# Hybrid attention block: tiles of one-pass matmuls moved to one address residue, a second accumulator in the second norm, and ScalarE's order written out at the end

## The chip, the cores and the metric

The kernel runs on one core of one Trainium2 chip. The metric is the device time of one execution in microseconds (us), as the median over several runs.

## The reference

One layer of a streaming encoder on 1024 frames (T) of 1024 features (D), all in float32:

```python
h = rmsnorm(x, norm1_g)
qa, ka, va, qb, kb, vb = split(h @ w_in)             # 8 heads of 64 in each group
ya = chunked_attention(qa, ka, va, rel_bias)          # softmax over a band of 9 chunks of 64 frames
yb = stick_breaking_attention(qb, kb, vb)             # causal, no softmax
x = x + concat(rmsnorm(ya, norm_a_g), rmsnorm(yb, norm_b_g)) @ w_out
u = causal_depthwise_conv3(rmsnorm(x, norm2_g) @ w_ffn_in, conv_w) + conv_b   # 2 x 2816 columns
gate, val = split(u)
x = x + (silu(gate) * val) @ w_ffn_out
return rmsnorm(x, final_g)
```

`rmsnorm(x, g)` is x / sqrt(mean of x² over the features + 1e-6) × g.

## The kernel before

**Layout and products.** Activations lie transposed, features on the 128 partitions and frames along the free axis: a [1024, 1024] array is 8 tiles of [128, 1024]. Nearly every matrix product is made in three matmuls of the one-pass type fp32r: each operand is split into a rounded high part (copied by ScalarE) and a low part (the rest, subtracted by VectorE or GpSimd, `sub`, L132), and high×high, high×low and low×high are added up in PSUM. The weight piece is the stationary operand (128 columns of it), the activations are the moving one (512 columns). One tile's "product" in the stages below is 4 input tiles × 3 = 12 matmuls into one bank of [128, 512].

**Stages.** 
- *start*: the first norm and the value projection (`all_v`, L506) in seven products p = 1, 2, 5, 6, 7, 3, 4 of a Strassen-like scheme with 48 matmuls each, then the queries and keys of group B in four rounds (`early`, L1255): each round seven products of 12 matmuls.
- *b* and *a*: the two attention groups, with projections in between as filler.
- Output projection (`out_part`, L154) with residual, second norm, and the first up projection.
- *ffn*: the up projection in pairs of column tiles. `up_pair` (L1875) makes, for f = 3 to 21, the seven products a11, s1, s2, a12, s3, s4, a22 of 12 matmuls, while VectorE and ScalarE finish the previous pair (conv taps at L1899, bias and last tap at L1893) and make the pieces of the next one. The down projection follows (L2386, 70 entries of 12 matmuls), and `last_down` (L2249 ff.) does the last two of 22 feature tiles, the residual and the final norm in three parts of 3, 3 and 2 blocks of 128 frames (`LAST`).

**Where tiles lie.** Tiles come from pools, one after another in each partition's bytes. The long-lived pools `cp`, `wp` and `kp` hold most operands; each stage has a pool of its own behind them. The first tile of all, `cst`, holds 40 columns of constants (160 bytes); the stage pool of *ffn* begins with `conv`, 176 columns (704 bytes: three conv taps, the bias and some columns of zeros); that of *start* begins with the tiles `r0` to `r3`, `l0`, `l1`, then `ms` (64 bytes) and `c`. By these sizes, tiles of `cp`, `wp` and `kp` begin at 192 modulo 256 bytes; in *start* `r0` to `l1` begin at 64 and `c` at 128; in *ffn* everything behind `conv` begins at 128.

**The second norm.** For each half g of the frames and each feature tile d, `out_part` makes the projection, the residual is added, and `norm_part` / `x2_part` squares the tile on ScalarE (L1681, L1686) and adds the squares up: the first goes directly into an accumulator, the others into a temporary that GpSimd adds (L1687). `own = KT - len(accs)` is the last d that goes through GpSimd; with one accumulator in the half that is d = 7. `totals` (L171) sums over the partitions with small matmuls against ones, one group for each accumulator; `root` (L163) takes the square root on ScalarE and the reciprocal on VectorE; `across` (L184) spreads it over the partitions by transposes. Then for each tile VectorE multiplies (L1706), ScalarE copies the high part (L1709) and VectorE subtracts. `second_norm` is a generator: the first `next` does `rstd`, the second the transposes and the first tile, and each further one a tile. The first half is stepped by the loop over d of the second half, with 0, 1, 1, 1, 1, 1, 2, 2 steps; the second half's `rstd` is written at n = 6 in `up_first`'s loop over (ct, k) (L1928), its further steps from n = 10 on.

**Order.** TensorE's order is the one written in the code throughout, as are those of VectorE, ScalarE and GpSimd and of the loads, until `last_down`. There, VectorE and GpSimd still follow the code, and ScalarE's order is left to the scheduler. In `last_down` each part does for d = 0 to 7 the products, an add on VectorE (L2313), the square into one of 1, 2 or 4 accumulators, and for some d a multiplication by the final gain on ScalarE (L2293 in the third part, L2320 in the others). `final` of a part is a generator that runs inside the next part: at d = 2 `rstd` (its root needs an ACT_TABLE_LOAD in the first part), then the transposes, ScalarE's copy of their result (L2270) and VectorE's multiplies (L2284) one by one with an output DMA each. For the third part, VectorE and GpSimd multiply pairs of tiles (L2275).

Of the kernel before, what the change touches and what calls it, by code (L numbers as in the profile page):

```python
# [9 lines left out]
F32 = mybir.dt.float32  # L10
# [6 lines left out]
P = 128  # L17
T = 1024
D = 1024
KT = 8  # L20
G = 2
GW = 512
FF = 2816
NF = FF // P
# [31 lines left out]
LATE_W = ("wo6", "wo7")  # L56
H2_TAGS = {0: ("x6", "x7"), 1: ("x0", "x1"), 2: ("x2", "x3")}

C_G1, C_G2, C_GY, C_GF, C_TB, C_W0, C_W1, C_W2, C_CB = 0, 8, 16, 24, 32, 40, 84, 128, 172
C_N = 216  # L60


def r32(ap):
# [4 lines left out]
def tile_hybrid_block(  # L68
# [13 lines left out]
    nc = tc.nc  # L82
    V, S, PE, GP = nc.vector, nc.scalar, nc.tensor, nc.gpsimd
# [31 lines left out]

    cst = one("cst", "cst", shape=(P, C_W0))
    nc.scalar.dma_start(cst, consts[:, :C_W0])
    conv = {}

    def c1(off):  # L120
        t, off = (cst, off) if off < C_W0 else (conv["t"], off - C_W0)
        return t[:, off : off + 1]

    ident = one("ident", "ident", shape=(P, P))
# [23 lines left out]
    def rows(g):  # L148
        return slice(g * GW, (g + 1) * GW)
# [27 lines left out]
    def rstd(sums, c0, c1, width, rn, name):  # L177

        root(rn[:, c0:c1], totals(sums, c1 - c0, name), width)
# [19 lines left out]
    with tc.tile_pool(name="kp", bufs=2) as kp:  # L199
# [43 lines left out]
        for k in range(KT):  # L243
            a, b = hpair(k, "hT")
# [3 lines left out]
        def all_v():  # L248
# [11 lines left out]

            def own(tag, dt=F32R, shape=(P, T)):
                return pools["sbuf"].tile(list(shape), dt, tag=tag, name=f"v_{tag}", bufs=1)

            w_areas = (
                (area(own("r0"), own("r1")), area(own("r2"), own("r3"))),
# [39 lines left out]
            bring_row(1)  # L305
            nc.sync.dma_start(v_d[0][P:, 4 * T - GW :], consts[:1, C_N:])

# [1166 lines left out]
        with stage("b"):  # L1474
# [11 lines left out]
            for b in range(len(items) + 3):  # L1486
                cur, h = items[b] if b < len(items) else (None, 0)
                step = (RATE_B / 16 if cur else DRAIN) / (1.5 if b < 2 else 3)
                if cur:
                    n = cur.n  # L1490
# [11 lines left out]
                if ending:  # L1502
                    pair, ending = ending, []
                    n = pair[0].n
# [88 lines left out]
        for b in range(len(blocks) + 2):  # L1593
# [6 lines left out]
            if cur and cur.i == 0:  # L1600
                n, p = cur.n, cur.p
# [6 lines left out]
            if b in (2, 3):  # L1608
                g = b - 2
# [14 lines left out]
            if cur and cur.p == 3 and cur.i in (3, 4):  # L1624
                g = cur.i - 3
# [62 lines left out]

        wa = []
        acc0 = kp.tile([P, 2 * GW], F32, tag="v", name="n2_acc0", bufs=4)  # L1690
        accs = {0: [acc0[:, rows(0)]]}
        hp2 = [None] * KT

        def second_norm(g):
# [32 lines left out]
        for g in range(G):  # L1727
            if g == 1:
                at1 = wp.tile([P, 2 * GW], F32, tag="wr", name="n2_at1", bufs=1)
                accs[1] = [at1[:, rows(0)]]  # L1730
            for d in range(KT):
                if (g, d) == (0, 5):
                    up_r = {ct: kp.tile([P, D], F32, tag="v", name=f"up{ct}_r", bufs=4) for ct in (0, NF)}
                    for ct in (0, NF):
                        nc.sync.dma_start(up_r[ct], w_up[ct])
                if g == 0 and d % 2 == 0:
                    wa.append(take(w_late if d > 3 else w_ready))
                for _ in out_part(*wa[d // 2], 0, d, g, "pa"):
                    pass
                flow.emit(x2_chains[d, g])  # L1740
                if (g, d) == (0, 3):
                    fetch(w_late, kp, ("x10", "x11"), 1)
                    flow.drain()
                first = {1: 0, 3: NF}.get(d) if g else None
                if first is not None:
                    first_high(first)
                nc.sync.dma_start(x2_d[d][:, rows(g)], x2[d][:, rows(g)])
                norm_part(d, rows(g), accs[g], kp, f"n2_{g}")
                if first is not None:
                    first_low(first)  # L1750
                for _ in range((0, (0, 1, 1, 1, 1, 1, 2, 2)[d])[g]):
                    next(norms[0])
        a_stage.__exit__(None, None, None)

    with stage("ffn"):
        fp = pools["sbuf"]
        conv["t"] = fp.tile([P, C_N - C_W0], F32, tag="conv", name="conv", bufs=1)

        def at(slot, name, dt=F32):
            pool = wp if slot == "wr" else fp if slot[0] == "s" else cp  # L1760
# [150 lines left out]
        def up_first():  # L1911

            o = {(g, ct): zbank(f"u{ct}_{g}") for g in range(G) for ct in (0, NF)}
            c = {f: (at("s7", f"cg{f}"), at("s8", f"cv{f}")) for f in (0,)}
            raws = [at(t, f"up1_r{i}") for i, t in enumerate(("s9", "s10"))]
            for t, ct in zip(raws, (1, NF + 1)):
                nc.sync.dma_start(t, w_up[ct])
            nc.sync.dma_start(conv["t"], consts[:, C_W0:C_N])
            load_up(2)
            w1 = [[], []]  # L1920

            def weights1(n):
                w1[n] += [piece(raws[n][:, r], f"up1_{n}{i}") for i, r in enumerate(halves)]

            def plain(o, w, k, g, first, last, r=None):
                wh, wl = w
                for i, (a, t) in enumerate(((wh, 0), (wh, 1), (wl, 0))):
                    PE.matmul(  # L1928
                        o, a[:, cols(k if r is None else r)], hp2[k][t][:, rows(g)],
                        start=first and i == 0, stop=last and i == 2,  # L1930
                    )

            n = 0
            for ct in (0, NF):
                for k in range(KT):
                    if n == 6:
                        next(norms[1])
                        weights1(0)
                    if n >= 10:
                        next(norms[1])  # L1940
                    plain(o[0, ct], up_w[ct], k, 0, k == 0, k == KT - 1)
                    n += 1
                S.copy(c[0][ct // NF][:, lo], o[0, ct])
            for _ in norms[1]:
                pass
            weights1(1)
            sums = combine_all("t2")
            for _ in range(3):
                next(sums)
            for i, k in enumerate(K_ORDER[1]):  # L1950
                for ct in (0, NF):
                    plain(o[1, ct], up_w[ct], k, 1, i == 0, i == KT - 1)
            for ct in (0, NF):
                S.copy(c[0][ct // NF][:, hi], o[1, ct])
            done, left = Finish(0, *c[0]), Left(2)
            done.first("g")
            for _ in sums:
                pass
            done.first("v")
            left.whole_high()  # L1960
            done.taps("g")
            left.make("s1")
            left.whole_low()
            done.taps("v")
            done.silu()
            left.make("s2")
            left.make("s4")
            c[1] = (at("s7", "cg1"), at("s8", "cv1"))

            def product_1(n, bank):  # L1970
                os = [bank(f"u1_{n}{g}") for g in range(G)]
                for k in range(KT):
                    for g in range(G):
                        plain(os[g], w1[n][k // 4], k, g, k == 0, k == KT - 1, k % 4)
                return lambda: [S.copy(c[1][n][:, rows(g)], os[g]) for g in range(G)]

            copy = product_1(0, med)
            for _ in combine_all("t3"):
                pass
            done.gate()  # L1980
            left.high("s4")
            left.high("s2")
            copy()
            done = Finish(1, *c[1])
            left.low("s4")
            left.low("s2")
            done.first("g")
            left.make("s3")
            product_1(1, pj)()
            for _ in combine_all("t4"):  # L1990
                pass
            load_up(3)
            done.taps("g")
            for w in ("s3", "s1", "a22"):
                left.high(w)
            for w in ("s3", "s1", "a22"):
                left.low(w)
            load_up(4)
            return done
# [249 lines left out]
        def last_down(chunk, x2):  # L2249
            accs = [  # L2250
                at(where[1 + i // 2, 2 + i % 2], f"n3_acc{i}") for i in range(4)
            ]
# [5 lines left out]
            def final(c0, c_end):  # L2258
                sl = slice(c0 * P, c_end * P)
                last = accs[: {3: 1, 6: 2, 8: 4}[c_end]]  # L2260
                rstd([a[:, sl] for a in last], c0, c_end, D, rn2, f"n3_{c0}")
                if c_end == KT:
                    for d in range(4, KT):
                        gain(d)
                yield
                n = (c_end - c0) * P
                ob = zbank(f"n3_{c0}_rb")[:, :n]
# [23 lines left out]
            def gain(d):  # L2291
                y = res[d // 4][:, d % 4, :]
                S.activation(y, y, AF.Copy, scale=c1(C_GF + d))  # L2293
# [109 lines left out]
            do()  # L2403
        own_order.__exit__(None, None, None)
        loads_order.__exit__(None, None, None)
        with tc.manual_schedule(engines={V.engine, GP.engine}):
            last_down([2 * NP, 2 * NP + 1], x2n)
    pe_order.__exit__(None, None, None)

# [1 line left out]
def _layout(inputs):  # L2411
    import numpy as np

    def a(name):
        return np.asarray(inputs[name])

    def cols(v):
        return v.reshape(-1, P).T

    def tiles(w):  # L2420
# [9 lines left out]
    conv_w = a("conv_w")[0]  # L2430
# [1 line left out]
        [  # L2432
            cols(a("norm1_g")[0]), cols(a("norm2_g")[0]), cols(a("norm_a_g")[0]),
            cols(a("norm_b_g")[0]), cols(a("final_g")), np.broadcast_to(rel[:, -1], (P, 8)),
            cols(conv_w[0]), cols(conv_w[1]), cols(conv_w[2]), cols(a("conv_b")[0]),
            np.zeros((P, GW), np.float32),
        ],
        axis=1,
    )
# [32 lines left out]
```

## Time and profile before

| | us |
|---|---|
| median of 3 runs | 1217.43 |
| lowest, highest | 1216.38, 1219.96 |
| the profiled execution | 1217.9 |
| its span | 1216.2 |

Mean granted TensorE clock in the profiled execution: 0.996 of full speed. In the profile, PE is TensorE's matmuls and PEld its weight loads, DVE VectorE, ACT ScalarE, POOL GpSimd, SP the engine that issues most DMAs; L and a number is a line of the kernel. A row of the chain of work has the start, the time and the instruction group that stood on the path; a row of a timeline has the start, the time, engine, line, operation, output and inputs, and in brackets the idle time ahead of it and who ended that.

### The profile page before, as it was taken

Reading aid. Unit: us, or ns where it says so; the run is one execution under the profiler, and the core shown is the slowest. Engines: PE = TensorE matmul, PEld = TensorE weight load, DVE = VectorE, ACT = ScalarE, POOL = GpSimd, SP = SyncE. Lnnn points to the kernel's source line nnn. Section 1 sums busy time; section 2 is a strip of 40 time slices with the busy share of each in tenths; the row PEclk is TensorE's granted clock in tenths of the full one; section 3 lists DMA queues with packets and bytes.
Section 4 is the critical chain, followed back from the end, with each engine's and each line's share of the span. In section 5 each row is a group of like instructions: output and inputs, shape, how many; then the busy total and the mean of one; then the engine's idle time right before and its main releaser. Section 6 shows DMA issues by size and latency. Waiting matters only on the chain.

```text
span 1216.2 us, 17043 instructions
## 1 busy us (share of the span) xinstructions
PE 1195.9 (98%) x6252; PEld 984.3 (81%) x6252; DVE 927.5 (76%) x1382; ACT 685.3 (56%) x1252; POOL 161.9 (13%) x163
## 2 busy tenths in 40 slices
PE   9999999999999999999999999999999999999997
PEld 6788888888878778787888888888888888888886
DVE  7957649878666767468997777768677779979885
ACT  7865436766667667334665554555555555444425
POOL 0001031102211111342000000000000023132035
PEclk9999999999999999999999999999999999999998
DMA  9467577777478831142132222132221295520003
GB/s 329 136 210 265 177 236 197 217 182 187 144 182 253 227 110 53 38 153 107 39 112 92 87 70 99 58 105 71 85 87 70 85 369 237 190 88 1 1 1 139
DMA packets 73793, 166.91 MB, mean 137 GB/s; under 512 B 7783, under 2 KB 23271, under 8 KB 73710
## 3 DMA queue, kind: packets, MB, share of 16 engines
q1 hardware_dynamic: 73566, 165.81, 43.1%
q8 instruction: 49, 0.80, 0.3%
q14 instruction: 34, 0.28, 0.1%
q10 hardware_dynamic: 144, 0.02, 0.0%
HBM read 118.60 MB, written 47.20 MB: 136 GB/s over the span
## 4 chain that ended last, share of the span: by engine, by line
PE 88%; DVE 6%; ACT 3%; DMA 1%; issue 1%; POOL 0%; SPq 0%; DVEq 0%; ACTq 0%
PE u_c L1875 9%; PE u_a L1875 9%; PE u_e L1875 9%; PE dz L2386 8%; PE u_b L1875 5%; PE dm L2386 4%; PE dj L2386 4%; PE v_x L506 4%; PE pb L154 3%; PE pa L154 3%; PE k_p L154 3%; PE v_y L506 3%; PE yb L1011 3%; PE tpb L997 3%; PE q_p L154 3%; PE yy L1144 2%
## 5 line engine op out<-in xcount | busy, mean ns | idle before, releaser
L970 DVE TENSOR_TENSOR_SCAN acts<-zb,first 128x128 f32<-128x128 f32 (+7 forms) x64 | 86.5, 1351 | 17.6 <-ACT zb L979 17.4
L1899 DVE SCALAR_TENSOR_TENSOR vt<-cv,conv,vt 128x1023 f32<-128x1023 f32 (+1 forms) x44 | 58.3, 1325 | 2.2 <-ACT vt L1893 1.5
L1899 DVE SCALAR_TENSOR_TENSOR gt<-cg,conv,gt 128x1023 f32<-128x1023 f32 (+1 forms) x44 | 57.4, 1305 | 1.5 <-ACT gt L1893 0.7
L132 POOL TENSOR_TENSOR dx_0wl<-dr,dx_0wh 128x512 fp32r<-128x512 f32 x1 | 1.4, 1357 | 414.6 <-ACT dx_0wh L2142 414.6
L979 ACT ACTIVATE zb<-zb 128x128 f32<-128x128 f32 (+7 forms) x64 | 41.0, 640 | 26.1 <-PE zb L962 26.1
L1089 ACT ACTIVATE pa<-sa,sta 128x640 f32<-128x640 f32 (+4 forms) x64 | 42.7, 668 | 18.1 <-DVE sta L1080 14.6
L1893 ACT ACTIVATE gt<-cg,conv 128x1024 f32<-128x1024 f32 x22 | 27.4, 1244 | 39.9 <-DVE cg L1767 39.8
L1001 ACT COPY tb<-tpb 128x128 f32<-128x128 f32 (+3 forms) x96 | 43.0, 484 | 6.2 <-PE tpb L997 5.5
L1125 ACT COPY pta<-tpa 128x512 f32<-128x512 f32 (+3 forms) x80 | 36.9, 483 | 13.3 <-PE tpa L1121 13.1
L997 PE MATMUL tpb<-ident,acts 128*128 128x128 f32 x288 | 43.3, 277 | 0.0
L1080 DVE TENSOR_REDUCE sta<-sa 128x1 f32<-128x640 f32 (+4 forms) x64 | 41.8, 655 | 1.3
L1764 DVE TENSOR_TENSOR up_r<-up_r 128x512 f32<-128x512 f32 x60 | 41.3, 688 | 0.8
L1121 PE MATMUL tpa<-ident,pa 128*128 128x128 f32 x240 | 37.9, 277 | 1.1 <-ACT pta L1125 1.1
L997 PEld LDWEIGHTS tpb<-ident,acts 128*128 128x128 f32 x288 | 33.0, 140 | 6.4 <-issue 2.6
L1077 DVE TENSOR_TENSOR sa<-sa,bias 128x256 f32<-128x256 f32 (+1 forms) x64 | 26.4, 414 | 11.0 <-PE sa L1062 7.8
L1121 PEld LDWEIGHTS tpa<-ident,pa 128*128 128x128 f32 x240 | 27.9, 140 | 7.9 <-issue 2.6
L2063 ACT COPY u_b<-u_a 128x512 f32<-128x512 f32 x19 | 10.8, 571 | 38.6 <-PE u_a L1875 38.6
L1144 PE MATMUL yy<-pta,v 128*64 128x256 f32 (+1 forms) x288 | 29.7, 349 | 0.0
L1687 POOL TENSOR_TENSOR n_acc<-n_acc,n_sq 128x384 f32<-128x384 f32 (+2 forms) x24 | 25.6, 1065 | 28.9 <-ACT n_sq L1686 28.1
L1011 PE MATMUL yb<-tb,dv 128*64 128x128 f32 x448 | 29.2, 273 | 0.0
L1764 DVE TENSOR_TENSOR dr<-dr,dr 128x512 f32<-128x512 f32 x40 | 28.7, 739 | 0.0
L154 PE MATMUL pb<-yh,wo_h 128*128 128x512 f32 x64 | 27.0, 421 | 1.8 <-DVE x L1219 1.8
(1400 smaller groups left out, 4011.0 us busy)
## 6 DMA issues: line engine op xcount, KB each, us to landing
up_r<-in_w_up_dram SPq DMA_DIRECT2D x44, 512.0 KB, 3.5
act<-vt SPq DMA_DIRECT2D x22, 512.0 KB, 2.6
dr<-in_w_dn_dram SPq DMA_DIRECT2D x20, 512.0 KB, 7.0
dr<-act SPq DMA_DIRECT2D x20, 512.0 KB, 7.9
wv<-in_w_v_dram SPq DMA_DIRECT2D x16, 256.0 KB, 5.4
xin<-in_xT_dram SPq DMA_DIRECT2D x16, 256.0 KB, 5.4
row<-in_x_rows_dram SPq DMA_DIRECT2D x16, 256.0 KB, 2.6
raw<-in_w_in_dram SPq DMA_DIRECT2D x8, 512.0 KB, 5.2
```

Source lines behind the costliest of these rows:

```text
L154: PE.matmul(o, w[:, sl], t[:, rows(g)], start=first and i == 0, stop=last and i == 2,)
L506: PE.matmul(bank[j], t[:, cols(j)], w, start=p in (1, 5) and k == 0 and i == 0, stop=k == 3 and i == 2, skip_group_check=True,)
L970: V.tensor_tensor_scan(out=a[:, :w], data0=z, data1=first[:, :w], initial=1.0, op0=ALU.mult, op1=ALU.max,)
L997: PE.transpose(tp[:, cols(b)], self.a[h][:, cols(b0 + b)], ident)
L1001: mine.append(flow.add(on_s(m * P, lambda o=o, tp=tp: S.copy(o, tp))))
L1011: PE.matmul(yy[HS[h], :], (d if j else v)[:, off : off + 64], self.at[h][:, self.c0[h] + j * P : self.c0[h] + (j + 1) * P], start=j == 0, ...
L1121: PE.transpose(tp[:, cols(b)], self.pr[src][:, cols(c)], ident)
L1144: PE.matmul(yy[HS[h], q], v[:, c * P + h * 64 : c * P + (h + 1) * 64], t[:, h], start=j == 0, stop=j == len(parts) - 1, skip_group_check=True,
L1764: eng.tensor_tensor(out=out, in0=a, in1=b, op=ALU.subtract)
L1875: PE.matmul(o, w[:, cols(k)], t, start=start and k == 0 and i == 0, stop=k == 3 and i == 2, skip_group_check=True,)
L1899: V.scalar_tensor_tensor(out=t[:, : T - lag], in0=o[:, lag:], scalar=c1(c + ct), in1=t[:, : T - lag], op0=ALU.mult, op1=ALU.add,)
L2386: PE.matmul(o[m], w[:, cols(m)], t, start=i in (0, 1, 4, 5) and p == ps_[0] and j == 0, stop=p == ps_[-1] and j == 2, skip_group_check=True,)
```

## The change

It does three things.

1. *Placement.* The conv bias moves from the stage's tile to the constants loaded at the start, so `cst` has 88 columns (352 bytes, 192 more) and the stage tile, now `taps`, holds the three taps in a tile of 192 columns (768 bytes), of which 132 are loaded. In *start* a tile `front` of 128 bytes that nothing reads or writes stands ahead of `r0`. By the sizes, tiles of `cp`, `wp` and `kp` then begin at 128 modulo 256; in *start* `r0` to `l1` at 128 and `c` at 192; in *ffn* everything behind `taps` at 128. In the other stages tiles keep their distances.
2. *Second norm.* Each half has two accumulators, so d = 7's square goes directly into the second one, and `totals` does two groups of matmuls. The first half is stepped 1, 1, 1, 1, 1, 1, 1, 2 times over d, and the second half's `rstd` is written at n = 5.
3. *The end.* ScalarE's order in `last_down` is the one written. Gains 4 and 5 of the third part stand ahead of its `rstd`, 6 and 7 behind it (before, all four behind it).

```diff
-C_G1, C_G2, C_GY, C_GF, C_TB, C_W0, C_W1, C_W2, C_CB = 0, 8, 16, 24, 32, 40, 84, 128, 172
-C_N = 216
+C_G1, C_G2, C_GY, C_GF, C_TB, C_CB, C_W0, C_W1, C_W2 = 0, 8, 16, 24, 32, 40, 88, 132, 176
+C_N = 220
...
+            own("front", F32, (P, 32))
...
-        accs = {0: [acc0[:, rows(0)]]}
+        accs = {0: [acc0[:, rows(i)] for i in range(2)]}
...
-                accs[1] = [at1[:, rows(0)]]
+                accs[1] = [at1[:, rows(i)] for i in range(2)]
...
-                for _ in range((0, (0, 1, 1, 1, 1, 1, 2, 2)[d])[g]):
+                for _ in range((0, (1, 1, 1, 1, 1, 1, 1, 2)[d])[g]):
...
-        conv["t"] = fp.tile([P, C_N - C_W0], F32, tag="conv", name="conv", bufs=1)
+        taps["t"] = fp.tile([P, 192], F32, tag="taps", name="taps", bufs=1)
...
-            nc.sync.dma_start(conv["t"], consts[:, C_W0:C_N])
+            nc.sync.dma_start(taps["t"][:, : C_N - C_W0], consts[:, C_W0:C_N])
...
-                    if n == 6:
+                    if n == 5:
                         next(norms[1])
...
+                if c_end == KT:
+                    gain(4)
+                    gain(5)
                 rstd([a[:, sl] for a in last], c0, c_end, D, rn2, f"n3_{c0}")
                 if c_end == KT:
-                    for d in range(4, KT):
-                        gain(d)
+                    gain(6)
+                    gain(7)
...
-        with tc.manual_schedule(engines={V.engine, GP.engine}):
+        with tc.manual_schedule(engines={V.engine, S.engine, GP.engine}):
             last_down([2 * NP, 2 * NP + 1], x2n)
```

The host's layout of the constants follows the new columns.

More of the change, by code (lines that the diff above doesn't have):

```diff
@@ L117, in tile_hybrid_block @@
     nc.scalar.dma_start(cst, consts[:, :C_W0])
-    conv = {}
+    taps = {}
     def c1(off):
-        t, off = (cst, off) if off < C_W0 else (conv["t"], off - C_W0)
+        t, off = (cst, off) if off < C_W0 else (taps["t"], off - C_W0)
         return t[:, off : off + 1]
@@ L2434, in _layout @@
             cols(a("norm_b_g")[0]), cols(a("final_g")), np.broadcast_to(rel[:, -1], (P, 8)),
-            cols(conv_w[0]), cols(conv_w[1]), cols(conv_w[2]), cols(a("conv_b")[0]),
-            np.zeros((P, GW), np.float32),
+            cols(a("conv_b")[0]), np.zeros((P, C_W0 - C_CB - 2 * NF), np.float32),
+            cols(conv_w[0]), cols(conv_w[1]), cols(conv_w[2]), np.zeros((P, GW), np.float32),
         ],
```

## The prediction

> **What bounds the kernel now.** I read the page first, then the chain of work that ended last stage by stage, and the timelines of TensorE, VectorE and ScalarE where the chain leaves TensorE.
>
> ```profile
> span 1216.2 us, 17043 instructions
> ...
> PE 1195.9 (98%) x6252; PEld 984.3 (81%) x6252; DVE 927.5 (76%) x1382; ACT 685.3 (56%) x1252; POOL 161.9 (13%) x163
> ...
> PE 88%; DVE 6%; ACT 3%; DMA 1%; issue 1%; POOL 0%; SPq 0%; DVEq 0%; ACTq 0%
> ```
>
> TensorE is busy 98% of the span and carries 88% of the chain. So two things can shorten the kernel: each matmul takes less time, or one of the few stretches where the chain runs through VectorE and ScalarE (9% together) gets shorter. The change tries the first in four stages and the second in two places. The profiled execution took 1217.9 us (its span and 1.7 around it), 0.5 above the median of 1217.43; I make the sum against 1217.9 and take it from the median at the end.
>
> **Part 1, the placement.** First, one period of the channel mixer on the chain (start, time, output tile; each piece is one product of 12 matmuls):
>
> ```profile
> 627.87 2.73 PE u_b L1875 x12
> 630.60 2.76 PE u_a L1875 x12
> 633.36 2.76 PE u_c L1875 x12
> 636.12 2.75 PE u_e L1875 x12
> 638.87 2.75 PE u_c L1875 x12
> 641.62 2.73 PE u_a L1875 x12
> 644.35 2.75 PE u_e L1875 x12
> 647.10 2.73 PE u_b L1875 x12
> ```
>
> The products follow each other without a gap: 647.10 − 627.87 = 19.23 us for seven. They differ a little, and the difference follows the code: u_a at 641.62 (a11) takes both operands from tiles of the old pools, u_b (s2) both from the stage's own pool; both take 2.73. u_e (s1, s4) and u_c at 638.87 (a22) take one from each: 2.75. From the tile sizes, the stage's tiles lie 64 bytes off the others modulo 256: its pool and the old ones begin at the same residue, its first tile has 704 bytes, and that is 64 short of three times 256. u_a at 630.60 (a12) has both alike and still takes 2.76, but it comes right after a product at another residue; so does u_c at 633.36, whose right operands are mixed. What alike operands cost with no such change before them, the first product of the up projection shows, where all tiles are of the old pools (start, time, operation):
>
> ```profile
> 553.36 0.39 PE L1928 MATMUL u<-h2h,up_wh 128*128 128x512 f32 x1
> ...
> 556.76 0.39 PE L1928 MATMUL u<-h2h,up_wh 128*128 128x512 f32 x1
> ```
>
> From the first to the sixteenth are 15 intervals in 3.40 us: 226.7 ns each, 2.72 a product. The change makes the stage's first tile 768 bytes (a multiple of 256) and puts every tile of the mixer at one residue, so I price the period at 7 × 2.72 = 19.04 instead of 19.23. Pairs f = 3 to 21 are 19 periods: 0.19 × 19 = **−3.6**. The other end: at 2.73, the price of the best products in the period, 0.12 × 19 = −2.3; if a12 keeps its 2.76 for another reason and s3 too, 0.06 × 19 = −1.1. Nothing else must run faster for this: in these rows the chain stays on TensorE, and VectorE, 76% busy over the span, is not on it. For f = 0 to 2, I count nothing, since the stretch up to 608 waits for VectorE (part 2).
>
> The same holds at the start, where own tiles lie 128 apart from the others:
>
> ```profile
> 51.09 11.45 PE v_y L506 x48
> 62.53 10.90 PE v_x L506 x48
> 73.44 11.19 PE v_y L506 x48
> ...
> 96.45 2.73 PE ea L1255 x12
> ...
> 101.97 2.80 PE eb L1255 x12
> 104.76 2.74 PE ea L1255 x12
> ...
> 113.05 2.77 PE ec L1255 x12
> ```
>
> Here the same 48 matmuls take 10.90 when both operands are in the old pools (product 3) and 11.45 and 11.19 when the weights' pieces are in own tiles (7 and 4). The `early` products show 2.74 and 2.80 beside each other, and seven of them 113.05 + 2.77 − 96.45 = 19.37. After the change six take 2.72; the seventh reads its low pieces in `c`, which ends 64 bytes off, so about 2.75 as above: 19.07. Four heads' rounds: 0.30 × 4 = **−1.2**. Of `all_v`, products 7 and 4 give about 0.3 each, **−0.6** (for 7, whose 11.45 holds a wait too, I take no more than for 4). What the products ahead of 51 would give I count at nothing, because VectorE sets the pace there:
>
> ```profile
> 45.00:50.00 5.00, 5.00 (x24) 4.14 (x23) 5.00 (x9) 4.16 (x11) 0.00 (x0) 1.00 0.48 148
> ```
>
> The columns are the stretch, its length, then busy time with counts of TensorE's matmuls, weight loads, VectorE, ScalarE and GpSimd: VectorE is busy all 5.00 us. If this cover were not there, two more products would give 0.6.
>
> The down projection, two pieces of the chain, an early one and the last:
>
> ```profile
> 1028.86 13.76 PE dz L2386 x60
> ...
> 1165.87 13.65 PE dz L2386 x60
> ```
>
> Between their starts lie 600 matmuls (50 entries of 12): 137.01 / 600 = 228.4 ns. At 226.7, 840 of them gain 1.4; where pieces are only just ready some of it is lost, and I take **−1.2**. Other fp32r matmuls keep their places: the attention stages' tiles all move by the same 192 bytes, so nothing there changes, and the larger constant load at the start and the conv taps' load are one DMA each before and after. Sum of part 1: −6.6. Bounds: −2.5 (the mixer at −1.1, the rest by half) to −8.
>
> The Trainium skill ("TensorE: Matmul & The Clock Gate", "Step-by-step: what each phase is for") says that streaming operand and weight load have read ports of their own, and that loading weights takes no read bandwidth from the running matmul. By it where the two lie would not matter and part 1 would be zero. The trace does not bear it out: the same 48 matmuls take 10.90 and 11.19.
>
> **Part 2, the second norm.** With two accumulators, the last square of each half goes from ScalarE straight into the second, and GpSimd's last add goes; the totals take 16 small matmul records instead of 8. What bounds it now, on the chain and in the windows:
>
> ```profile
> 535.20 0.79 PE n_ms L171 x8
> ...
> 557.28 0.64 ACT n_sq L1686
> 557.98 1.61 POOL n_at L1687
> 559.64 1.05 PE n_ms L171 x8
> 560.69 4.45 PE u L1928 x12
> 565.14 0.45 PE n_rb L184 x4
> ...
> 565.62 0.76 DVE x L1706
> ...
> 608.21 3.02 PE u_b L1875 x12
> ```
>
> ```profile
> 562.00:564.00 2.00, 2.00 (x7) 1.52 (x6) 1.29 (x2) 1.29 (x3) 0.00 (x0) 0.50 1.05 405
> ```
>
> TensorE gets to the totals, waits until GpSimd has added (557.98 + 1.61 = 559.59), then does four blocks of three matmuls ahead of the transposes; these 12 take 4.45 instead of 12 × 0.227 = 2.72, because the granted clock is down (the last but two column: 0.50 of full speed). VectorE's multiplies follow at 565.62, and from there to 608.21 the chain is VectorE nearly without a gap, so what is won at 565.14 is won at 608. After: the first half's totals cost 0.79 more, while its first step comes one tile earlier and h2 with it, so the up projection starts about 0.5 later (553.9). Five blocks at 0.68 instead of six stand ahead of the totals: 557.3. The square ends at 557.92; the first eight records run before that, the second eight end 0.8 to 1.0 after it, 558.9. Five blocks then stand ahead of the transposes, 3.4: 562.3, at the latest some 0.4 more by a piece of h2 that isn't ready: 562.7. So **−2.4**. If the clock falls as before, 1.73 of it is lost: −0.7. If nothing waits, 562.0: −3.1. The upper end I don't take, since TensorE's small records at 557 to 559 also leave the array idle; the clock I take as granted, since the wait that came before its fall goes.
>
> **Part 3, ScalarE in program order at the end.** `last_down` leaves ScalarE's order to the scheduler now; after, its instructions stand as written. Rows of the timeline (start, time, engine, line; in brackets the idle time before and its releaser):
>
> ```profile
> 1191.15 1.28 ACT L163 ACT_TABLE_LOAD   x1
> ...
> 1192.61 0.51 ACT L1686 ACTIVATE n_sq<-x2n 128x384 f32<-128x384 f32 x1
> ...
> 1193.55 0.48 ACT L2270 COPY n_rbs<-n_rb 128x384 f32<-128x384 f32 x1 [0.43 <-PE n_rb L184]
> ...
> 1194.06 0.61 DVE L2284 SCALAR_TENSOR_TENSOR x2n<-x2n,cst,n_rb 128x384 f32<-128x384 f32 x1 [0.71 <-ACT n_rbs L2270]
> ...
> 1206.07 0.51 ACT L2293 ACTIVATE res<-res,cst 128x256 f32<-128x256 f32 x1
> ...
> 1207.33 0.40 ACT L1681 ACTIVATE n_acc<-res 128x256 f32<-128x256 f32 x1
> 1208.43 0.26 ACT L163 ACTIVATE rn<-n_ms,eps 128x2 f32<-128x2 f32 x1 [0.16 <-PE n_ms L171]
> ```
>
> The scheduler now puts the first part's root, with its table load, ahead of the second part's square of d = 2 (1192.61). As written the root comes behind that square, which can't start before its add: the table load moves from 1191.15 to about 1192.1, +0.95. The copy (1193.55) comes behind the square of d = 3, +0.4. VectorE's multiply waits for this copy, and from 1194.06 on VectorE goes from multiply to add without idling, so 1.35 carries on. In the third part the second root and its copy come behind the gains of d = 2 and 3: a gain starts 0.42 after its neighbour ((1207.33 − 1206.07) / 3 for a gain, a square, a gain), so +0.45 each, +0.9. Given back: the squares of d = 5 to 7 no longer alternate with gains 4 to 6, so the last square comes two gains sooner, −0.9; but gains 4 and 5 now stand ahead of the last root, of which the totals on TensorE hide half, +0.4, and 6 and 7 ahead of the last copy, +0.2. Sum: 0.95 + 0.4 + 0.9 − 0.9 + 0.6 = **+2.0**. Bounds: −0.5, if the first root's delay is taken up by waits for products in the second part and only the end counts; +5, if the table load and each of the four gains and squares named stand on the path in full (1.28 + 8 × 0.45). I take the value between, by the 1194.06 row, on which VectorE waited for ScalarE.
>
> **Sum.** −6.6 − 2.4 + 2.0 = −7.0: 1210.9 for the profiled execution, **1210.4** for the median. About 0.3%, 3.7 us, is what a measurement of this kernel can tell from no change: faster means under 1213.8, slower over 1221.1.
>
> **Rivals.**
> First: the placement pays nothing; the small differences between products come from their order or from who else reads, and alike tiles take 19.23 a period as before. For it: a12, alike, takes 2.76. Against: 10.90 beside 11.19 for the same work, and 226.7 ns in the alike stretch. Then −2.4 + 2.0 = −0.4: 1217.0, no change. That the change misses its aim by a tile that ends elsewhere would come out the same, in part.
> Second: the order at the end costs nothing, because what VectorE waits for is set by the products and their banks anyway, or because fewer alternations repay it. For it: ScalarE idles 0.43 and 0.16 before two of its rows there, so has room. Against: the idle 0.71 on VectorE is ScalarE's. Then −9.0 to −9.5: 1208.2.
> Third, the other side: program order ties VectorE to ScalarE throughout the end. If at each of the 16 steps of parts two and three the next multiply or add waited for a square (0.51) and a gain (0.51), the end would be 16 × 1.02 = 16 longer: −9.0 + 16 = +7, 1224.4. It decides from 12.7 us on (9.0 + 3.7). Against it: an add needs only its product and bank, and a multiply the copy; neither reads a square or gain of its own part.
>
> **How the numbers follow.** The forecast with its terms in their bounds: 0.70; the first rival 0.12, the second 0.15, the third 0.03. The range leaves out the last and most of the first, about 2 in 10 with what lies beyond the bounds: 1207.2 (both the placement at −7.5 and the norm at −2.7, the end at 0) to 1214.4 (the placement at −4, the norm at −1, the end at +2). Faster: 0.70 less a twentieth for terms at their low ends, and 0.15: 0.82. Same: 0.12 and that rest, 0.15. Slower: 0.03.
>
> **What would show it.** Right: u_a to u_e all at 2.72 and periods of 19.04; `early` rounds of 19.1; 60 products of the down projection in 13.60; n_ms on the chain behind a square, not behind GpSimd, and the VectorE multiply of the second half at about 563; the table load at 1192 when counted from the same start of the end, and the end from the first part's table load to the last output about 2 longer, less the shift. Wrong: periods of 19.1 or more; a granted clock of 0.5 again ahead of the transposes; VectorE's multiply in the end waiting no longer than 0.7.

## The result and the profile after

The changed kernel takes 1211.55 us (median of 4 runs, 1211.29 to 1212.13), the kernel before, run again beside it, 1218.43: 6.9 us less, a ratio of 0.9945 with the 95% interval 0.9928 to 0.9962. The forecast was 1210.4 with a range of 1207.2 to 1214.4. The profiled execution of the changed kernel has a span of 1210.4, 5.8 less than the one of before; it took 1212.13, 0.6 above its median, where the one of before lay 0.5 below the 1218.43.

One period of the channel mixer in the chain of waits of the changed kernel (start, time, output tile, line; L1875 is L1877 now):

```profile
623.43 2.72 PE u_b L1877 x12
626.15 2.72 PE u_a L1877 x12
628.87 2.72 PE u_c L1877 x12
631.59 2.72 PE u_e L1877 x12
634.31 2.72 PE u_c L1877 x12
637.03 2.72 PE u_a L1877 x12
639.75 2.72 PE u_e L1877 x12
642.47 2.72 PE u_b L1877 x12
```

Every product takes 2.72, a12 (u_a at 626.15) and s3 (the u_c behind it) too, which took 2.76 before; a period is 642.47 − 623.43 = 19.04. The start of the kernel and the down projection, from the same view:

```profile
50.78 11.17 PE v_y L508 x48
61.95 10.88 PE v_x L508 x48
...
95.52 2.72 PE ea L1257 x12
...
111.84 2.77 PE ec L1257 x12
114.61 2.73 PE ea L1257 x12
...
1157.39 13.60 PE dz L2391 x60
```

A round of `early` is 114.61 − 95.52 = 19.09 instead of 19.37. Its last product, which reads low pieces in the tile `c`, is the only one above 2.73: `c` still lies 64 bytes off. Sixty matmuls of the down projection take 13.60 instead of 13.65.

The second norm, in the chain, with the same places as before:

```profile
530.24 1.68 PE n_ms L171 x16
...
552.21 3.40 PE u L1930 x15
555.61 1.68 PE n_ms L171 x16
557.29 3.57 PE u L1930 x15
...
561.33 0.76 DVE x L1708
...
603.91 3.01 PE u_b L1877 x12
```

GpSimd is gone from the chain: the totals follow fifteen matmuls at once, and the fifteen behind them take 3.57, at a granted clock of 1.00 (twelve took 4.45 before). VectorE's first multiply of the second half comes at 561.33 instead of 565.62.

And the end (timeline of ScalarE, then of TensorE):

```profile
1183.62 1.28 ACT L163 ACT_TABLE_LOAD   x1
...
1186.36 0.46 ACT L2275 COPY n_rbs<-n_rb 128x384 f32<-128x384 f32 x1
...
1201.31 0.42 ACT L1683 ACTIVATE n_acc<-res 128x256 f32<-128x256 f32 x1 [0.30 <-DVE res L2318]
1201.63 0.89 ACT L2298 ACTIVATE res<-res,cst 128x256 f32<-128x256 f32 x2
1202.54 0.26 ACT L163 ACTIVATE rn<-n_ms,eps 128x2 f32<-128x2 f32 x1
```

```profile
1195.90 0.54 PE L184 MATMUL n_rb<-ident,rn 128*128 128x128 f32 x3 [1.52 <-DVE rn L164]
1196.20 4.62 PE L2313 MATMUL dnl<-lx,lw 128*128 128x256 f32 x24
```

These need a common zero: the last 60 matmuls of the down projection begin at 1165.87 before and at 1157.39 after. Counted from there the table load moved from 25.28 to 26.23, +0.95, and the copy from 27.68 to 28.97, +1.3, both as priced. But TensorE now waits 1.52 ahead of the second part's transposes, and the 24 matmuls behind them, which belong to the third part's products, take 4.62. The kernel before had:

```profile
1202.57 0.54 PE L184 MATMUL n_rb<-ident,rn 128*128 128x128 f32 x3 [0.44 <-DVE rn L164]
1202.86 3.11 PE L2308 MATMUL dnl<-lx,lw 128*128 128x256 f32 x24
```

The windows of the changed kernel say why the 24 take longer (stretch, length, busy time of PE, PEld, DVE, ACT and POOL, granted clock, then the DMA engines' share and GB/s):

```profile
1193.50:1195.50 2.00, 0.88 (x7) 0.67 (x6) 0.00 (x0) 1.94 (x6) 1.13 (x2) 1.00 0.22 78
...
1197.50:1199.50 2.00, 2.00 (x11) 2.00 (x11) 1.84 (x4) 0.51 (x3) 0.33 (x2) 0.50 0.20 75
```

The granted clock fell to 0.50 behind the wait; what that carries of the longer end, the experiments show. Where the time went, by the starts of the same matmuls in both timelines (the first of each output; us won or lost within the stage):

| stretch | forecast | changed | placement alone |
|---|---|---|---|
| value projection and first query | −0.6 | −0.9 | −0.5 |
| `early`, four rounds | −1.2 | −1.1 | −1.1 |
| attention stages | 0 | −0.2 | +0.5 |
| output projection, second norm, f = 0 and 1 | −2.4 | −2.05 | 0.0 |
| mixer from s2 of f = 2 on | −3.6 | −3.8 | −3.8 |
| down projection | −1.2 | −0.5 | −1.3 |
| the end | +2.0 | +2.8 | +0.3 |
| sum | −7.0 | −5.8 | −5.9 |

The last column is the first experiment's. The −0.5 of the down projection holds a wait of 0.5 for ScalarE at its beginning that isn't in the profile of the placement alone; what the placement gives there is −1.0 to −1.3.

### The profile page after: what moved, and what is told of

The parts are those of the page before. It is cut to its first block, busy times and chain, and to the rows that moved or that the text cites. A ratio compares the mean times of both kernels' runs of the same rounds, so it can differ in the third digit from the quotient of the medians.

```text
span 1210.4 us, 17073 instructions
## 1 busy us (share of the span) xinstructions
PE 1189.5 (98%) x6268; PEld 986.1 (81%) x6268; DVE 925.2 (76%) x1382; ACT 685.6 (57%) x1252; POOL 159.9 (13%) x161
## 4 chain that ended last, share of the span: by engine, by line
PE 87%; DVE 7%; ACT 3%; DMA 1%; issue 1%; SPq 1%; DVEq 0%; ACTq 0%
PE u_a L1877 9%; PE u_c L1877 9%; PE u_e L1877 9%; PE dz L2391 8%; PE u_b L1877 5%; PE dj L2391 4%; PE dm L2391 4%; PE pa L154 3%; PE pb L154 3%; PE v_x L508 3%; PE k_p L154 3%; PE yb L1013 3%; PE tpb L999 3%; PE q_p L154 3%; PE yy L1146 2%; PE v_y L508 2%
## 5 line engine op out<-in xcount | busy, mean ns | idle before, releaser
L1901 DVE SCALAR_TENSOR_TENSOR vt<-cv,taps,vt 128x1023 f32<-128x1023 f32 (+1 forms) x44 | 58.2, 1323 | 3.3 <-ACT vt L1895 2.5
L1901 DVE SCALAR_TENSOR_TENSOR gt<-cg,taps,gt 128x1023 f32<-128x1023 f32 (+1 forms) x44 | 56.5, 1285 | 1.6 <-ACT gt L1895 0.8
L1895 ACT ACTIVATE gt<-cg,cst,taps 128x1024 f32<-128x1024 f32 x22 | 27.4, 1244 | 35.9 <-DVE cg L1769 35.8
L154 PE MATMUL k_p<-hTh,k_h 128*128 128x512 f32 x64 | 27.6, 432 | 0.0
```

Source lines behind the costliest of these rows:

```text
L154: PE.matmul(o, w[:, sl], t[:, rows(g)], start=first and i == 0, stop=last and i == 2,)
L1901: V.scalar_tensor_tensor(out=t[:, : T - lag], in0=o[:, lag:], scalar=c1(c + ct), in1=t[:, : T - lag], op0=ALU.mult, op1=ALU.add,)
```

## The experiments

My theory: the parts add up, the placement gives its part by distance modulo 256, and the end loses by ScalarE's places in the order. The rivals: the stages run faster for what the norm hands on, or the end is longer because it is reached sooner. Four kernels, first each part of the change alone, or without it. Medians, with the ratio to the kernel before in runs beside it (the row "before" is that of the four; the changed kernel's ratio is to its own 1218.43); "end" is the time from the start of the last 60 down matmuls to the end of the span. The expectations count the end from the close of these 60, 13.6 us later.

| kernel | median us | ratio, 95% interval | end us |
|---|---|---|---|
| before | 1218.27 | | 50.3 |
| changed | 1211.55 | 0.9945 (0.9928 to 0.9962) | 53.0 |
| placement alone | 1210.8 | 0.9942 (0.9930 to 0.9955) | 50.6 |
| norm alone | 1216.65 | 0.9987 (0.9979 to 0.9996) | 49.9 |
| end alone | 1220.2 | 1.0024 (1.0015 to 1.0033) | 52.9 |
| changed, end as before | 1209.31 | 0.9933 (0.9920 to 0.9945) | 49.9 |

**Changed, with the end as before.**

```diff
-                if c_end == KT:
-                    gain(4)
-                    gain(5)
                 rstd([a[:, sl] for a in last], c0, c_end, D, rn2, f"n3_{c0}")
                 if c_end == KT:
-                    gain(6)
-                    gain(7)
+                    for d in range(4, KT):
+                        gain(d)
...
-        with tc.manual_schedule(engines={V.engine, S.engine, GP.engine}):
+        with tc.manual_schedule(engines={V.engine, GP.engine}):
```

> The changed kernel with its third part undone (ScalarE free again in the end, gains 4 to 7 behind the root). From the last 60 products of the down projection to the last output the end took 36.7 us before and 39.4 after. If the written order of ScalarE is what costs these 2.7, the end is back at 36.7 and the kernel takes 1208.8 us (1211.55 - 2.7). Rival: the end is longer because everything ahead of it comes 8.5 sooner and something that does not move (a transfer, GpSimd) is then late; it stays at about 39.4 and the kernel at 1211.5.

The end is 49.9, 3.1 shorter than the changed kernel's, though it is reached as early. The rival by which an earlier arrival costs falls: it's the order. In the median, 2.2 us less; the intervals of the two ratios overlap.

**Placement alone** (the constants, `front` and `taps` of the change in the kernel before).

> The kernel before with the placement alone. By the starts of the same matmuls in both traces the stages with moved tiles gained 0.9 (value projection), 1.1 (early), 3.7 (mixer) and 1.15 (down projection) and lost 0.7 on the way from the mixer to the down projection: -6.2, about 1212.2 us, if the gain is the placement's. Rival: the placement does nothing by itself and the stages run faster because the second norm hands over sooner or in another state; then about 1218 and periods of 19.23 in the mixer.

The stages with moved tiles won −6.7 in the table above, −6.3 in the changed kernel, and the mixer's share is −3.8 without any of the norm's part.

**Norm alone** (accumulators, steps and n = 5 in the kernel before).

> The kernel before with the second norm's part alone (two accumulators, new steps, root at n = 5). If the parts add up, -2.1 (from -2.2 ahead of the norm to -4.3 at the first product of the mixer's chain): 1216.3 us. Rival, by which the mixer's gain hangs on this part: -6 or more, under 1212.5.

The stretch from the output projection's second group to the mixer gains 2.06 in its profile, the mixer nothing; the ratio 0.9987 is −1.6. So the mixer's gain does not hang on this part.

**End alone** (the two edits of `last_down` in the kernel before).

> The kernel before with the written order of ScalarE in the end alone. If the order costs by itself, +2.7: 1221.1 us, with an end of 39.4 and the granted clock at 0.5 while TensorE does the last 24 products of the third part. Rival: it only costs where the rest comes sooner; then 1218.4 and an end of 36.7.

52.9, 2.6 longer, and the same wait and fall: 1.52 idle, and 4.61 for 24 matmuls. The measured +0.24% (0.15 to 0.33) is 2.9 us. By ratios the three parts alone give −0.58 − 0.13 + 0.24 = −0.47%, and the changed kernel has −0.55% with an interval of ±0.17.

**The step of the part before ahead of the square.** ScalarE's order stays written, but at d = 2 and 3 the root and the copy of the part before stand where the scheduler had put them:

```diff
+                    if d in (2, 3) and todo:
+                        go(1)
                     x2_part({d: y}, d, slice(0, y.shape[1]), [a[:, sl] for a in last], None, f"n3_{c0}", sqs[d % 2][:, :GW])
...
-                        go((d > 1) + 2 * (d == KT - 1))
-                    elif d in (2, 3, 4):
+                        go((d > 3 or d > 1 and c0 == 0) + 2 * (d == KT - 1))
+                    elif d == 4:
                         go(1)
```

> The changed kernel with ScalarE still in written order in the end, but at d = 2 and 3 the step of the part before (root, then transposes and copy) is written ahead of the square, not behind it. If it is these places that cost, the first table load comes 11.6 us after the last 60 products of the down projection (12.6 in the changed kernel), VectorE's multiply 14.5 after (15.9), TensorE's wait ahead of the third part's transposes shrinks from 1.5 to about 0.4, its clock stays up, and the end takes 36.7 or, if gains behind the last squares help too, 35.8: 1208 to 1209 us. Rival: any fixed order costs ScalarE what the scheduler had gained by interleaving; then over 1210.5.

It takes 1208.45 (0.9922, 0.9908 to 0.9935), the lowest median of all, though its interval overlaps those of the changed kernel and of the one with the end as before. From its chain:

```profile
1156.65 13.60 PE dz L2393 x60
```

Its end is 1206.6 − 1156.65 = 49.95, and in the timelines the table load comes 25.25 after that row, as in the kernel before, and TensorE waits 0.56 ahead of the second part's transposes and does the 24 in 3.12:

```profile
1181.90 1.28 ACT L163 ACT_TABLE_LOAD   x1
```

```profile
1193.21 0.54 PE L184 MATMUL n_rb<-ident,rn 128*128 128x128 f32 x3 [0.56 <-DVE rn L164]
1193.51 3.12 PE L2313 MATMUL dnl<-lx,lw 128*128 128x256 f32 x24
```

So a written order need not cost; these two places do. The further gain that the expectation allowed, from gains that stand behind the last squares, did not show: 49.95 against 49.86 with the scheduler's order.

**TensorE kept busy in its wait.** The changed kernel with 12 matmuls more, whose result is not read:

```diff
+                if c0 == 3:
+                    warm = zbank("warm")[:, :2 * P]
+                    (wh, _), (xh, _) = last_w[chunk[0]], last_x[chunk[0]]
+                    for i in range(12):
+                        PE.matmul(warm, wh[:, cols(0)], xh[:, 6 * P :], start=i == 0, stop=i == 11)
                 across(ob, rn2, c0, c_end)
```

> The changed kernel with 12 more matmuls of 256 columns, whose result nobody reads, ahead of the second part's transposes, in the 1.5 us in which TensorE waits there. In the changed kernel the 24 products behind this wait take 4.6 us with the granted clock at 0.5, in the kernel before 3.1 with the clock at 1. If the fall of the clock after an idle TensorE is what holds the last adds, and through them the last squares, the 24 take 3.1 to 3.6 and the kernel 1210.0 to 1210.6. Rival: they are slow because each waits for its bank, which an add frees; then nothing changes, 1211.5.

```profile
1194.13 1.60 PE L2277 MATMUL warm<-lx,lw 128*128 128x256 f32 x12
1195.83 0.54 PE L184 MATMUL n_rb<-ident,rn 128*128 128x128 f32 x3
1196.13 3.11 PE L2318 MATMUL dnl<-lx,lw 128*128 128x256 f32 x24
1199.92 1.95 PE L171 MATMUL n_ms<-ones,n_acc 128*128 128x2 f32 x16 [0.68 <-POOL n_acc L1689]
```

The 24 take 3.11 again. That the extra matmuls kept the clock up is not shown by this, since it can stay up without them. Three of the kernels below have the changed kernel's end and such a wait, 1.40 to 1.54, and in their profiles the 24 take 3.12: the one with one accumulator and two with a longer first tile of the mixer, of N = 208 and N = 256 columns. Here is N = 256:

```profile
1195.57 0.54 PE L184 MATMUL n_rb<-ident,rn 128*128 128x128 f32 x3 [1.54 <-DVE rn L164]
1195.86 3.12 PE L2313 MATMUL dnl<-lx,lw 128*128 128x256 f32 x24
1199.66 1.95 PE L171 MATMUL n_ms<-ones,n_acc 128*128 128x2 f32 x16 [0.68 <-POOL n_acc L1689]
```

The granted clock is 1.00 over these 24. So the clock made them slow, not the banks. But it is not what makes the end long. At full clock the totals wait 0.68 for GpSimd's last add of squares, which follows ScalarE, and the end is 52.7 in N = 256 and with one accumulator and 52.3 with the extra matmuls, against 53.0 in the changed kernel. The time with them, 1211.83 (0.9949, 0.9937 to 0.9962), shows no gain that can be measured. The clock carries 0.4 to 0.7 of the end's 2.7; the order of ScalarE carries the rest, 2.0 or more.

**The distance modulo 256**: three kernels that differ from the changed one only in the length of the mixer's first tile, each with a single execution, the profiled one (1221.16, 1216.28 and 1211.42 us for N = 208, 240 and 256).

```diff
-        taps["t"] = fp.tile([P, 192], F32, tag="taps", name="taps", bufs=1)
+        taps["t"] = fp.tile([P, N], F32, tag="taps", name="taps", bufs=1)   # N = 208, 240, 256
```

> The changed kernel with the first tile of the mixer's stage 64 bytes longer (832 bytes): its tiles lie 64 bytes off the others again, the other way round than before. If the distance modulo 256 sets the pace, periods go from 19.04 back to 19.2 and the down projection's 60 products from 13.60 to 13.7: 3.5 to 5 us more between the mixer's first product and the last part. Rival: the gain came from the smaller number of columns loaded or the bias in the constants; then 19.04.

> The changed kernel with the first tile of the mixer's stage 192 bytes longer (960 bytes). Modulo 256 its tiles then lie 64 bytes ahead of the others, as in the kernel before, where the tile has 704 bytes. If the signed distance modulo 256 is what counts, periods are 19.23 as before (19.40 with 64 bytes the other way) and the groups of 60 at 13.7. Rival, that the plain distance counts, the larger the dearer: above 19.40.

> The changed kernel with the first tile of the mixer's stage 256 bytes longer (1024 bytes). If only the distance modulo 256 counts, periods stay at 19.04 and the groups of 60 at 13.60. If it is modulo 512 or more, they change, to 19.2 or above.

The chain of N = 208 (64 bytes more) and of N = 240 (192 more): s1 and s1 of the next pair, which reads one tile of each pool. Then s1 of N = 256 (256 more).

```profile
640.61 2.80 PE u_e L1877 x12
...
660.01 2.80 PE u_e L1877 x12
```

```profile
640.29 2.75 PE u_e L1877 x12
...
659.52 2.75 PE u_e L1877 x12
```

```profile
639.92 2.72 PE u_e L1877 x12
```

The periods are 19.40, 19.23 and, with every product at 2.72, 19.04. So 256 bytes are a whole turn; 192 more, which puts the tiles 64 below the others, gives the period of before to the hundredth; and 64 above costs twice as much (0.36 a period instead of 0.19). From the mixer to the end of the down projection the first of them loses 7.5 against the changed kernel's profile, more than the 3.5 to 5 I expected: I had taken the distance without its sign. The rivals, the smaller load and the plain distance, fall.

**Without `front`** (the changed kernel without the empty tile at the start).

```diff
-            own("front", F32, (P, 32))
```

> The changed kernel without the empty tile at the start, so that the own tiles of that stage lie 128 bytes off the others as in the kernel before. The early products go from 2.72 back to 2.74 to 2.80, a round of seven from 19.1 to 19.4, and the value projection's last 48 matmuls from about 10.9 to 11.2; the first projection behind the four rounds starts 1.6 to 2.0 us later than in the changed kernel, and the mixer stays at 19.04. If the start is paced by VectorE alone, nothing changes there.

```profile
99.27 2.79 PE ee L1255 x12
102.06 2.80 PE eb L1255 x12
```

The products of `early` are back at the times of before, and the first projection behind the four rounds starts at 173.87, as before (173.78) and 2.1 later than in the changed kernel (171.75). All profiles with the tile have this start at 171.75 to 172.23, all without it at 173.76 to 173.99. So this one unused tile of 128 bytes is worth about 2 us in the trace. The mixer stays at 19.04. The single execution took 1214.89; its end is 54.0, in which the 24 matmuls take 5.47.

**The two halves of the norm's part.** First, one accumulator again, with the new steps:

```diff
-        accs = {0: [acc0[:, rows(i)] for i in range(2)]}
+        accs = {0: [acc0[:, rows(0)]]}
...
-                accs[1] = [at1[:, rows(i)] for i in range(2)]
+                accs[1] = [at1[:, rows(0)]]
```

> The changed kernel with one accumulator in each half of the second norm again, its new steps kept (first half from d = 0, second half's root at n = 5). From the first matmul of the output projection's second group to the first product of the mixer's chain lie 98.6 us in the changed kernel and 100.6 in the one before. If the accumulator is what pays (no wait for GpSimd, no fall of the clock behind it), most of the 2.0 is lost, 100 or more: about 1213. Rival: the earlier steps pay, since five blocks instead of six stand ahead of the totals; then under 99.3 and about 1212. It may also come out above 100.6, since the totals now stand one block sooner and wait longer for GpSimd.

Then two accumulators with the old steps:

```diff
-                for _ in range((0, (1, 1, 1, 1, 1, 1, 1, 2)[d])[g]):
+                for _ in range((0, (0, 1, 1, 1, 1, 1, 2, 2)[d])[g]):
...
-                    if n == 5:
+                    if n == 6:
```

> The changed kernel with two accumulators, but the steps of before (first half 0, 1, 1, 1, 1, 1, 2, 2; second half's root at n = 6). If the accumulator is what pays, the stretch stays near 98.6 to 99.3 and the kernel near 1211.5 to 1212.2; by the rival, 100 or more and about 1213.

From the first matmul of the output projection's second group to the mixer's first product in the chain: 100.6 before, 98.6 changed, 99.2 with one accumulator, 101.7 with the old steps. The ratios, 0.9955 (0.9939 to 0.9972, 1213.36 us) and 0.9960 (0.9947 to 0.9973, 1214.49 us), overlap that of the changed kernel, so only the stretches of the profiles can decide. By its stretch the first kernel meets the rival (under 99.3), by its time (about 1212) it does not. The waits of TensorE with one accumulator, then with the old steps (us in total, times, longest), and the chain of the latter:

```profile
PE n_ms L171 <- POOL n_at L1689: 1.0, 1, 1.0
PE n_ms L171 <- POOL n_acc L1689: 0.8, 1, 0.8
```

```profile
PE u L1930 <- DVE h2l L132: 1.3, 1, 1.3
```

```profile
558.43 1.68 PE n_ms L171 x16
560.11 4.44 PE u L1930 x12
```

With one accumulator TensorE waits 1.8 for GpSimd, and its clock stays up. With the old steps no wait for GpSimd is left, but the 1.3 for the low part of h2 is, the totals cost twice the matmuls, and twelve matmuls behind them take 4.44 (granted clock 0.57 and 0.58 in the windows 560 to 562 and 562 to 564).

These stretches must not be compared as they stand, because the clock fell in two of them (before, old steps) and not in the others. The kernel with the end alone has the norm of before. Its profile shows the same two waits, yet its clock stays at 1.00 (timeline of TensorE, then the chain):

```profile
559.69 0.50 PE L1928 MATMUL u<-h2l,up_wh 128*128 128x512 f32 x1 [1.34 <-DVE h2l L132]
...
560.83 1.05 PE L171 MATMUL n_ms<-ones,n_at 128*128 128x2 f32 x8 [0.40 <-POOL n_at L1687]
```

```profile
561.88 2.87 PE u L1928 x12
```

Its twelve matmuls take 2.87 instead of 4.45, and its stretch is 99.0. So at the full clock the stretch is 99.0 before, 99.2 with one accumulator and the new steps, and 98.6 with both; with the fall it is 100.6 before and 101.7 with two accumulators and the old steps. Neither half of the change gains anything alone, both together gain 0.5, and the fall costs 1.6.

## Why the prediction was right, and where it was not

The time is inside the range, and the likeliest case was the one that came: placement and norm win, the end gives some back. That the median moved by 6.9 for a forecast of 7.0 is in part luck: in the profiles the stages add up to −5.8, and the norm's share hangs on a clock that does not fall in every execution.

*Placement*: right in mechanism and size. −6.6 forecast; the stages that it touches gave −6.7 in the kernel with the placement alone, −6.3 with the one wait in the changed kernel. The price of 2.72, read off an alike stretch in the up projection, held for every product of the period shown, and so did the guess that a12's 2.76 came from the product before it, not from its own tiles. The product with `c` came out at 2.77 where I took 2.75. The first rival, and the Trainium skill's statement on the two read ports as I had used it there ("TensorE: Matmul & The Clock Gate", "Step-by-step: what each phase is for"), do not hold for this kernel: the same products take 2.72, 2.75 or 2.80 by nothing but the distance of their tiles.

*Norm*: right in size, −2.05 in the changed kernel for −2.4. The clock that stays up is most of it, as I had it, but I most likely put its fall down to the wrong wait, and I took for granted that it falls in every execution of the kernel before. The timeline of TensorE before has both waits:

```profile
558.50 0.50 PE L1928 MATMUL u<-h2l,up_wh 128*128 128x512 f32 x1 [1.35 <-DVE h2l L132]
...
559.64 1.05 PE L171 MATMUL n_ms<-ones,n_at 128*128 128x2 f32 x8 [0.41 <-POOL n_at L1687]
```

The prediction showed the second alone, GpSimd's, and counted the first only as "h2" coming with its first step one tile earlier. Of the four profiles with the wait of 1.3 for h2, three show the fall behind it (before, placement alone, old steps) and one does not (end alone). Of the ten without that wait none falls there, not even the one that waits 1.8 for GpSimd. That points to the wait for h2, which the earlier steps remove, but it rests on single profiles; why the clock falls in some executions only stays open. Where the clock stays up in both, the whole part is worth 0.5.

*The end*: +2.8 in the profiles where I had +2.0. Counted from the common zero, the first copy came +1.3 for 1.35, and the second copy, which with its root now stands behind two gains, +2.4 (37.36 to 39.72) for 1.35 + 0.9. The step that failed is "the last square comes two gains sooner, −0.9". In the changed kernel the last square came 2.5 later (41.46 to 43.92), since its products ran at half the clock. In N = 256, where the clock stayed at 1.00, it came only 1.3 later (42.72), so the gains did give that back, but the root could not use it: the totals wait for GpSimd's last add, that of the square of d = 4. This square needs VectorE's add, which stands behind a multiply that waits for the second copy, so it starts 2.4 later at either clock (38.90 before, 41.25 changed, 41.26 in N = 256). The last copy then comes +2.0 in N = 256, the sum that I had, and +2.8 in the changed kernel, 0.7 of it by the clock. I did not ask what TensorE and GpSimd do while the root is late. The second rival, that the order costs nothing, falls with the end alone, 1.0024; the third, that it ties VectorE to ScalarE throughout, with its +16, too.

So the changed kernel is not the best one: with the scheduler's order at the end, or the written one with two steps put ahead, the medians are 1209.31 and 1208.45, and the ends 3.1 shorter in the profiles.

## What to carry to other kernels

A matmul stream that never waits can still run at several speeds: look for products of equal size with different times in the chain, sort them by which pools their two operands come from, and take the fastest stretch of the same kernel as the price to reach. When several waits end close together, the one that the chain shows last need not be the one whose removal pays; undo each edit by itself, and compare stretches of two profiles only where their granted clocks are alike. An order written by hand for an engine that "has room" has to be compared with the scheduler's at the few instructions that others wait for, and a wait of TensorE is priced with the matmuls behind it, since its clock may fall.

## What the runs showed of the hardware that I had not expected

The distance between the tiles of the weight piece and the activations counts with its sign modulo 256 bytes: with the mixer's own tiles, which hold the weight pieces of s1, 64 bytes above the others, s1 took 2.80, with 64 below 2.75, with 0 and 256 2.72; 128 apart, the products of `early` other than those into `ea` took 2.77 to 2.80. The two signs were read from products whose weight pieces lie in the own tiles; the reverse case was not read out. Behind a product at another residue an alike one, a12, took 2.76 instead of 2.72.

TensorE's granted clock fell to 0.50 behind a single wait of 1.52 us in the end, in the changed kernel as in the one with the end alone, and in the norm behind waits of 1.35 and 0.41. It does not fall each time: behind 1.54 in the end of N = 256, and behind 1.34 and 0.40 in the norm of the kernel with the end alone, it stayed at 1.00, as it did behind two waits of 0.8 and 1.0. What decides is not shown. The Trainium skill ("TensorE: Matmul & The Clock Gate", "HAM oscillation — how this bites in real kernels") speaks of idle gaps over about 3.4 us; the gaps here are less than half of that.
